# A transformer block in fp32 halves on one core: order of PE, ACT and DVE at the head and where one product's end meets the next product's start

## The chip, the cores and the metric

The kernel runs on one core of one Trainium2 chip. The metric is device time in microseconds (us) of one execution; the medians below are over the runs shown. A profiled execution also leaves a trace of every instruction on TensorE (PE, with weight loads as PEld), VectorE (DVE), ScalarE (ACT), GpSimd (POOL) and SyncE (SP, which here issues DMAs).

## What is computed

A block of depth 1 over 256 tokens of 2048 values (fp32): a gated feed-forward layer, a mixer (a recurrence of 16 heads plus a pooling branch, both gated), and a second feed-forward layer. Each is added to its input.

```python
def _rmsnorm(x, g):
    xf = x.astype(jnp.float32)
    y = xf * lax.rsqrt(jnp.mean(xf * xf, axis=-1, keepdims=True) + NORM_EPS)
    return (y * g.astype(jnp.float32)).astype(x.dtype)

def _swiglu(x, w_gate, w_up, w_down):
    return (jax.nn.silu(x @ w_gate) * (x @ w_up)) @ w_down
...
        f = _swiglu(_rmsnorm(h, ln_ffn1_pre[l]), ffn1_gate[l], ffn1_up[l], ffn1_down[l])
        h = h + MACARON_WEIGHT * _rmsnorm(f, ln_ffn1_post[l])
        mx = _hybrid_mixer(_rmsnorm(h, ln_mix_pre[l]), w_in[l], rwkv_mu[l], rwkv_w0[l],
...
        h = h + _rmsnorm(mx, ln_mix_post[l])
        f = _swiglu(_rmsnorm(h, ln_ffn2_pre[l]), ffn2_gate[l], ffn2_up[l], ffn2_down[l])
        h = h + MACARON_WEIGHT * _rmsnorm(f, ln_ffn2_post[l])
```

The hidden width of the feed-forward layers is 5632, `w_in` has 8480 columns, and the weights are read once.

## The kernel before

**Products.** Each fp32 factor is split into a high half and a low remainder (`xH`, `xL`, `wH`, `wL`), and `mm3` (L126 to L128) makes three matmuls of them: wH with xH, wL with xH, wH with xL. Tokens are 256, in two halves h of 128; a product of 512 output columns has two PSUM tiles of 128x512, one for each half, and runs over k, 128 rows of the weight at a time (16 for an input of 2048, 44 for 5632).

**Weights.** `load_w` issues a DMA on SP for two k of 512 columns (L105; 512 KB) into one of four buffers `w32`, then the cast `wH` on ACT (L108) and the difference `wL` on DVE (L109), each into one of five buffers; where `hold` is set the two go into units of the big pool (`kH`, `kL`) instead.

**Inputs.** `next_pre` makes the transposed input `uT` of the next layer. For each token half h and each 512 columns c it does a turn (`transpose_split`, L257 to L264): four 128x128 transposes on PE into one PSUM tile `tr`, and for each of the four a scaled copy `xH` on ACT (L263) and a scaled difference `xL` on DVE (L264), both reading `tr`. Sums of squares (`sumsq`, L290) and the factor rs (`rstd`) are put off into `s.late`: the product is scaled by rs when it is read out of PSUM.

**The end of a layer.** `post` makes four products of 512 columns. For the last (c == 3), `gemm_tok(trail=True)` does the last 16 k (TRAIL) first for half 0, then for half 1. When a half is done, its evacuation runs: sum of squares on ACT (L290), product with the gain `gb` into `fg` on DVE (L336), one small op on DVE (L349), the power -0.5 on POOL (L352), and four outputs on DVE (L355), each the 512 columns of one turn.

**The start of the next layer.** `gemm_tok(lead=True)` does the first ten k (STAG) of the next product by halves as well. The turns stand in `s.turns` with a time (TURNS, us of PE work after the evacuation), and `by_half` puts a turn among the products when its count has passed that time, or when the product needs it. This happens twice: from the first feed-forward layer to the mixer (`w_out` and `w_in` products around it) and from the mixer to the second feed-forward layer.

**Order.** The framework schedules instructions by priority and by its own model of time. From the trailing product on, `manual_schedule` holds PE alone to the source's order; ACT and DVE are in the scheduler's order there, with raised priorities (BOOST for the splits, FINISH for the turns and evacuations). At the head of the program nothing is held: x comes by eight DMAs on POOL's queue (L1040), the gain's rows and the weights on SP's, all eight turns are in the source ahead of the first product, and the parameters of the mixer are loaded (`setup_mixer`, 12 small DMAs on SP) before the first feed-forward layer.

Of the kernel before, what the change touches and what calls it, by code (L numbers as in the profile page):

```python
# [34 lines left out]
BOOST = 2000  # L35
FINISH = 4000
MM, MC = 0.2265, 0.12
NUNITS = 33
STAG = 10
TRAIL = 16  # L40
TURNS = [[3.8, 5.2, 6.8, 8.6], [4.2, 5.4, 8.8, 10.4]]
TB = 4
# [6 lines left out]
class Block:  # L49
    def __init__(s, tc, ctx):  # L50
        s.tc = tc
        s.nc = nc = tc.nc
        E = ctx.enter_context
        s.n = 0
        s.late, s.turns, s.held = [], [], None
        s.cp = E(tc.tile_pool(name="cp", bufs=1))
        s.wp = E(tc.tile_pool(name="wp", bufs=3))
        s.up = E(tc.tile_pool(name="up", bufs=NUNITS))
        s.tp = E(tc.tile_pool(name="tp", bufs=TB))
        s.sp = E(tc.tile_pool(name="sp", bufs=4))  # L60
        s.dp = E(tc.tile_pool(name="dp", bufs=1, space=bass.MemoryType.DRAM))
        s.pm = E(tc.tile_pool(name="pm", bufs=4, space=PSUM))
        s.pt = E(tc.tile_pool(name="pt", bufs=4, space=PSUM))
        s.ident = s.const([P, P], "ident")
        make_identity(nc, s.ident)
        s.mhalf = s.const([P, 16], "mhalf")
        nc.gpsimd.memset(s.mhalf, -0.5)
# [22 lines left out]

    def load_w(s, w, k0, nk, c0, cw, split=False, hold=False):
        nc = s.nc
        out = []
        step = 1 if split else max(1, 1024 // cw)
        for j in range(k0, k0 + nk, step):
            n = min(step, k0 + nk - j)
            w32 = s.wp.tile([P, 1024], F32, tag="w32", name=s.nm("w32"), bufs=W32_BUFS)
            if hold:
                wH, wL = s.unit(dt=F32R, p="kH"), s.unit(dt=F32R, p="kL")
            else:  # L100
                wH = s.wp.tile([P, 1024], F32R, tag="wH", name=s.nm("wH"), bufs=WS_BUFS)
                wL = s.wp.tile([P, 1024], F32R, tag="wL", name=s.nm("wL"), bufs=WS_BUFS)
            v, vH, vL = [t[:, :n * cw].rearrange("p (k c) -> p k c", k=n)
                         for t in (w32, wH, wL)]
            nc.sync.dma_start(out=v, in_=w[j * P:(j + n) * P, c0:c0 + cw]  # L105
                              .rearrange("(k p) c -> p k c", p=P))
            with s.tc.high_priority(offset=BOOST):
                nc.scalar.copy(vH, v)  # L108
                nc.vector.tensor_tensor(out=vL, in0=v, in1=vH.bitcast(F32), op=ALU.subtract)  # L109
            for i in range(n):  # L110
                out.append((j + i, vH[:, i], vL[:, i]))
        return out
# [16 lines left out]

    def gemm_tok(s, w, c0, at, KT, evac, lead=False, trail=False, first=False):  # L130
        pss = [s.pm.tile([P, 512], F32, tag="mm", name=s.nm("mm")) for _ in range(2)]

        def do(k, wH, wL, h):
            xH, xL = at(k)
            s.mm3(pss[h], xH[:, h * P:h * P + P], xL[:, h * P:h * P + P], wH, wL,
                  k == 0, k == KT - 1)

        def by_half(ws):

            for h in range(2):  # L140
                now = 0
                for k, wH, wL in ws:
                    while s.turns and (s.turns[0][0] <= now or s.turns[0][1] == (h, k // 4)):
                        s.turns.pop(0)[2]()
                    do(k, wH, wL, h)
                    now += 3 * MM
                s.turns = [(t - now, b, f) for t, b, f in s.turns]
                if k == KT - 1:
                    with s.tc.high_priority(offset=FINISH):
                        evac(h, pss[h])  # L150

        def both(k0, k1):
            for k2 in range(k0, k1, 4):
                for k, wH, wL in s.load_w(w, k2, min(4, k1 - k2), c0, 512):
                    do(k, wH, wL, 0)
                    do(k, wH, wL, 1)

        def held(k0, k1):
            ws = []
            for k in range(k0, k1, 2):  # L160
                ws += s.load_w(w, k, 2, c0, 512, first and k < 4, k - k0 >= STAG)
            return ws

        if trail:
            both(0, KT - TRAIL)
            ws = held(KT - TRAIL, KT)
            s.held = s.tc.manual_schedule(engines={mybir.EngineType.PE})
            s.held.__enter__()
            by_half(ws)
            return  # L170
        if lead:
            by_half(held(0, STAG))
            if s.held:
                s.held.__exit__(None, None, None)
                s.held = None
            while s.late:
                s.late.pop(0)()
        both(STAG if lead else 0, KT)
        with s.tc.high_priority(offset=BOOST):
            for h in range(2):  # L180
                evac(h, pss[h])

    def tok_g(s, w, c0, at, KT, evac):
# [49 lines left out]

    def rstd(s, ss, n):
        nc = s.nc
# [4 lines left out]
                                op0=ALU.mult, op1=ALU.add)  # L240
        r = s.small(1, "rs", bufs=8)
        nc.gpsimd.tensor_tensor(out=r, in0=t2, in1=s.mhalf[:, :1], op=ALU.pow)
        return r

# [46 lines left out]

    def ffn(s, wg, wu, wd, uT, rs, gpost, resid, emit, reload, first=False):
        nc = s.nc
        hT = s.new_T(NKF // 4)
        at = s.T_at(uT)
        for b in range(NKF // 4):
# [16 lines left out]

            s.gemm_tok(wg, b * 512, at, NKD, ev_g, lead=(b == 0), first=first and b == 0)
            s.gemm_tok(wu, b * 512, at, NKD, ev_u)
        s.post(wd, s.T_at(hT), NKF, gpost, 0.5, resid, emit, reload)

    def post(s, wd, at, KT, gpost, fac, resid, emit, reload):
# [11 lines left out]
        for c in range(4):  # L330
            def ev(h, ps):
# [7 lines left out]
                if c == 2:  # L339
# [5 lines left out]
                                            op1=ALU.add)  # L345
                if c < 3:
                    return
                r2 = s.small(1, "rt2", bufs=2)
                nc.vector.tensor_scalar(out=r2, in0=ss[h][:, 3:4], scalar1=kf,  # L349
                                        scalar2=part[h], op0=ALU.mult, op1=ALU.add)  # L350
                r = s.small(1, "rs", bufs=8)
                nc.gpsimd.tensor_tensor(out=r, in0=r2, in1=s.mhalf[:, :1], op=ALU.pow)  # L352
                for q in range(4):
                    o = cc_(fg[h], q)
                    nc.vector.scalar_tensor_tensor(out=o, in0=o, scalar=r, in1=resid(h, q),  # L355
                                                   op0=ALU.mult, op1=ALU.add)
                    emit(h, q, o, TURNS[h][q])
            s.gemm_tok(wd, c * 512, at, KT, ev, trail=(c == 3))

    def next_pre(s, gT):  # L360
        uT = s.new_T(4)
        ss = [s.small(4, "ss2") for _ in range(2)]
        rs = [None, None]

        def emit(h, c, ap, at=None):
            def turn():
                with s.tc.high_priority(offset=FINISH):
                    s.transpose_split(ap, uT, c, h, gT)

            def stat():  # L370
                s.sumsq(ap, ss[h][:, c:c + 1])
                if c == 3:
                    rs[h] = s.rstd(ss[h], D)
            s.late.append(stat)
            if at is None:
                turn()
            else:
                s.turns.append((at, (h, c), turn))
        return uT, rs, emit
# [640 lines left out]
def kernel(tc, x, ln_ffn1_pre, ln_ffn1_post, ffn1_gate, ffn1_up, ffn1_down,  # L1020
# [11 lines left out]
    with ExitStack() as ctx:  # L1032
# [3 lines left out]
        def at_tok(u):  # L1036
            return lambda h, c: u[h][c // 2][:, (c % 2) * 512:(c % 2) * 512 + 512]
        for h in range(2):
            for c in range(4):
                nc.gpsimd.dma_start(out=at_tok(xs)(h, c),  # L1040
                                    in_=x[0, h * P:h * P + P, c * 512:c * 512 + 512])
        gr = s.rtmp("g1rows")[:16, :P]
        nc.sync.dma_start(out=gr, in_=ln_ffn1_pre[0].rearrange("(k p) -> k p", p=P))
        ps = s.psum("pg1")
        nc.tensor.transpose(ps[:, :16], gr, s.ident[:16, :16])
        g1 = s.const([P, 16], "g1")
        nc.vector.tensor_copy(g1, ps[:, :16])

        uT, rs, pre = s.next_pre(g1)
        for h in range(2):  # L1050
            for c in range(4):
                pre(h, c, at_tok(xs)(h, c))
        s.setup_mixer(prm)
        uT2, rs2, pre2 = s.next_pre(s.col["ln_mix_pre"])
        xr = [[s.unit(p="xr") for _ in range(2)] for _ in range(2)]
# [10 lines left out]
        def emit1(h, c, ap, at):  # L1066
            pre2(h, c, ap, at)
            nc.gpsimd.dma_start(out=hsp[0, h, :, c * 512:c * 512 + 512], in_=ap)
        s.ffn(ffn1_gate[0], ffn1_up[0], ffn1_down[0], uT, rs, ln_ffn1_post[0],
              at_tok(xr), emit1, load_to(xr, lambda h: x[0, h * P:h * P + P]), first=True)  # L1070
        uT3, rs3, pre3 = s.next_pre(s.col["ln_ffn2_pre"])
        h1 = [[s.unit(p="h1") for _ in range(2)] for _ in range(2)]
# [8 lines left out]
        def emit(h, c, ap, at):  # L1081
            nc.sync.dma_start(out=out[0, h * P:h * P + P, c * 512:c * 512 + 512], in_=ap)
        s.ffn(ffn2_gate[0], ffn2_up[0], ffn2_down[0], uT3, rs3, ln_ffn2_post[0],
              at_tok(h2), emit, load_to(h2, lambda h: hsp[1, h]))
        s.held.__exit__(None, None, None)

# [31 lines left out]
```

## Time and profile before

| | |
|---|---|
| runs shown | 2119.78, 2122.1, 2122.66 us; median 2122.1 |
| the profiled execution | 2122.2 us, its span 2120.5 us |
| granted TensorE clock, mean | 0.995 |
| PE, PEld busy | 2091.8 us (99%), 1761.7 us (83%) |
| DVE, ACT, POOL busy | 1256.8 (59%), 1117.5 (53%), 76.2 us (4%) |
| HBM read, written | 396.69 MB, 8.39 MB |

How to read it: a line of a group has the source line, the engine, the operation, out<-in by the program's names, and the shapes; then busy time and mean ns; then the engine's idle time just before it and what ended most of it ("<-DVE xL L264": the instruction on DVE that wrote xL). A line of the timeline starts with the start and the length in us. PE's matmuls overlap, so a matmul of 0.39 us can start every 0.227 us; idle time and the distance from start to start say more than busy time. PEclk is the share of the full clock that was granted.

### The profile page before, as it was taken

Reading aid. Unit: us, or ns where it says so; the run is one execution under the profiler, and the core shown is the slowest. Engines: PE = TensorE matmul, PEld = TensorE weight load, DVE = VectorE, ACT = ScalarE, POOL = GpSimd, SP = SyncE. Lnnn points to the kernel's source line nnn. Section 1 sums busy time; section 2 is a strip of 40 time slices with the busy share of each in tenths; the row PEclk is TensorE's granted clock in tenths of the full one; section 3 lists DMA queues with packets and bytes.
Section 4 is the critical chain, followed back from the end, with each engine's and each line's share of the span. In section 5 each row is a group of like instructions: output and inputs, shape, how many; then the busy total and the mean of one; then the engine's idle time right before and its main releaser. Section 6 shows DMA issues by size and latency. Waiting matters only on the chain.

```text
span 2120.5 us, 28818 instructions
## 1 busy us (share of the span) xinstructions
PE 2091.8 (99%) x11077; PEld 1761.7 (83%) x11077; DVE 1256.8 (59%) x1588; ACT 1117.5 (53%) x1600; POOL 76.2 (4%) x169
## 2 busy tenths in 40 slices
PE   8999999999999999999999999999999999999998
PEld 6888888888888789989988788878888888888886
DVE  5555555555444555699789666565555555554444
ACT  6565555655444455465465444455655556554442
POOL 1000000000000000000110110000000000000000
PEclk9999999999999999999999999999999999999999
DMA  7666666577666656656456575666566665676664
GB/s 232 196 189 190 200 196 190 178 218 247 191 197 191 214 156 181 180 163 186 138 151 197 151 262 182 194 194 192 178 209 196 192 195 181 212 246 194 193 194 134
DMA packets 223605, 406.99 MB, mean 192 GB/s; under 512 B 13152, under 2 KB 49130, under 8 KB 223466
## 3 DMA queue, kind: packets, MB, share of 16 engines
q1 hardware_dynamic: 216937, 383.11, 59.6%
q0 software_dynamic: 6528, 22.02, 2.9%
q8 instruction: 87, 1.43, 0.3%
q14 instruction: 53, 0.43, 0.1%
HBM read 396.69 MB, written 8.39 MB: 191 GB/s over the span
## 4 chain that ended last, share of the span: by engine, by line
PE 76%; issue 20%; DVE 1%; DMA 1%; ACT 1%; POOL 1%; POOLq 0%; DVEq 0%; SPq 0%; ACTq 0%
PE mm L126 21%; PE mm L128 21%; PE mm L127 21%; PE mc L227 10%; DMA w<-in_ffn_gate_dram 1%; PE pA L840 0%; DVE fg L355 0%; DMA mb<-msp 0%; PE tr L257 0%; ACT x L283 0%; PE pU L936 0%; PE pY L971 0%; PE pSa L948 0%; PE pY L967 0%; PE pM L906 0%
## 5 line engine op out<-in xcount | busy, mean ns | idle before, releaser
L109 DVE TENSOR_TENSOR wL<-w,wH 128x1024 fp32r<-128x1024 f32 (+2 forms) x725 | 872.9, 1211 | 750.2 <-ACT wH L108 748.7
L108 ACT CAST wH<-w 128x1024 fp32r<-128x1024 f32 (+2 forms) x725 | 751.2, 1043 | 833.3 <-PE mm L128 675.6
L126 PE MATMUL mm<-wH,xH 128*128 128x512 f32 x2460 | 965.8, 393 | 6.8 <-ACT xH L263 6.7
L128 PE MATMUL mm<-wH,xL 128*128 128x512 f32 x2460 | 961.6, 391 | 4.4 <-DVE xL L264 4.4
L127 PE MATMUL mm<-wL,xH 128*128 128x512 f32 x2460 | 959.5, 391 | 0.0
L126 PEld LDWEIGHTS mm<-wH,xH 128*128 128x128 f32 x2460 | 463.8, 189 | 104.2 <-ACT xH L263 8.5
L128 PEld LDWEIGHTS mm<-wH,xL 128*128 128x128 f32 x2460 | 463.9, 189 | 102.4 <-DVE xL L264 6.1
L127 PEld LDWEIGHTS mm<-wL,xH 128*128 128x128 f32 x2460 | 463.9, 189 | 94.2
L227 PE MATMUL mc<-xH,wH 128*128 128x256 f32 x560 | 159.9, 285 | 0.0
L227 PE MATMUL mc<-xH,wL 128*128 128x256 f32 x560 | 158.6, 283 | 0.0
L227 PE MATMUL mc<-xL,wH 128*128 128x256 f32 x560 | 158.6, 283 | 0.0
L283 ACT COPY x<-T 32x256 f32<-32x256 f32 x352 | 141.9, 403 | 3.9
L227 PEld LDWEIGHTS mc<-xH,wH 128*128 128x128 f32 x560 | 106.1, 190 | 1.0
L227 PEld LDWEIGHTS mc<-xH,wL 128*128 128x128 f32 x560 | 106.1, 190 | 0.3
L227 PEld LDWEIGHTS mc<-xL,wH 128*128 128x128 f32 x560 | 106.2, 190 | 0.2
L302 ACT ACTIVATE sg<-mm,rs 128x512 f32<-128x512 f32 x44 | 30.1, 690 | 19.9 <-PE mm L128 19.9
L303 DVE SCALAR_TENSOR_TENSOR sg<-mm,rs,sg 128x512 f32<-128x512 f32 x44 | 31.6, 750 | 12.4 <-ACT sg L302 12.3
L333 POOL DMA_DIRECT2D gb<-in_ln_ffn_post_dram x4 | 2.2, 562 | 925.3 <-DVE xL L287 892.0
L290 ACT ACTIVATE junk<-mm 128x512 bf16<-128x512 f32 x24 | 14.3, 596 | 35.2 <-PE mm L128 35.2
L336 DVE TENSOR_TENSOR fg<-mm,gb 128x512 f32<-128x512 f32 x24 | 16.5, 692 | 25.1 <-ACT junk L290 25.1
L308 DVE SCALAR_TENSOR_TENSOR sg<-mm,rs,sg 128x512 f32<-128x512 f32 x44 | 30.9, 742 | 0.0
L273 DVE STREAM_TRANSPOSE T<-sg 128x512 f32<-128x512 f32 x44 | 30.8, 699 | 0.0
(244 smaller groups left out, 1087.6 us busy)
## 6 DMA issues: line engine op xcount, KB each, us to landing
w<-in_ffn_up_dram SPq DMA_DIRECT2D x176, 512.0 KB
w<-in_ffn_down_dram SPq DMA_DIRECT2D x176, 512.0 KB
w<-in_ffn_gate_dram SPq DMA_DIRECT2D x174, 512.0 KB
w<-in_w_in_dram SPq DMA_DIRECT2D x128, 512.0 KB
w<-in_w_out_dram SPq DMA_DIRECT2D x32, 512.0 KB
w<-in_w_proj_b_dram SPq DMA_DIRECT2D x16, 512.0 KB
w<-in_w_proj_a_dram SPq DMA_DIRECT2D x16, 512.0 KB
hsp<-fg POOLq DMA_DIRECT2D x16, 256.0 KB, 3.1
```

Source lines behind the costliest of these rows:

```text
L108: nc.scalar.copy(vH, v)
L109: nc.vector.tensor_tensor(out=vL, in0=v, in1=vH.bitcast(F32), op=ALU.subtract)
L126: nc.tensor.matmul(ps, aH, bH, start=start, stop=False)
L127: nc.tensor.matmul(ps, aH, bL, start=False, stop=False)
L128: nc.tensor.matmul(ps, aL, bH, start=False, stop=stop)
L227: s.nc.tensor.matmul(o, lh, rh, start=one and n == 0, stop=k == KT - 1 and n == 2, skip_group_check=True)
L273: s.nc.vector.transpose(out=T1[:, h * 512:h * 512 + 512], in_=src)
L283: nc.scalar.copy(dst[q * 32:q * 32 + 32, :, :, i], src[i * 32:i * 32 + 32, :, :, q])
L302: nc.scalar.activation(out=sg, in_=ps, func=AF.Sigmoid, scale=rs[h])
L303: nc.vector.scalar_tensor_tensor(out=sg, in0=ps, scalar=rs[h], in1=sg, op0=ALU.mult, op1=ALU.mult)
L308: nc.vector.scalar_tensor_tensor(out=sig[h], in0=ps, scalar=rs[h], in1=sig[h], op0=ALU.mult, op1=ALU.mult)
L336: nc.vector.tensor_tensor(out=cc_(fg[h], c), in0=ps, in1=cc_(gb, c), op=ALU.mult)
```

## The change

ACT and DVE join PE under `manual_schedule`. `gemm_tok` no longer issues the trailing and leading products at once but puts them into a queue (`s.items`, each with its PE time), and weight splits, evacuations, outputs and turns into a heap of events at counted times; `run` goes through both and issues everything in that order. The counted time of four transposes is TT, loads come AHEAD of their first product, and TURNS has new values. The head is written out in `head`, with PE, ACT, DVE and SP in the source's order: x and weights in one queue (SP's) in the order in which they are needed, the weights of the first product in units of their own, and a turn and a split at a time between the products. The sums of squares follow behind the head, `setup_mixer` behind the first block of the first feed-forward layer.

```diff
-TURNS = [[3.8, 5.2, 6.8, 8.6], [4.2, 5.4, 8.8, 10.4]]
+TT = 0.45
+AHEAD = (5.0, 6.0)
+TURNS = [[3.6, 4.7, 5.8, 6.9], [3.6, 4.6, 5.6, 6.6]]
...
+    def at(s, t, fn):
+
+        s.n += 1
+        heapq.heappush(s.events, (t, s.n, fn))
+
+    def run(s):
+
+        E = mybir.EngineType
+        with s.tc.manual_schedule(engines={E.PE, E.Activation, E.DVE}):
+            while s.items or s.events:
+                while s.events and (s.events[0][0] <= s.now or not s.items):
+                    heapq.heappop(s.events)[2]()
+                if s.items:
+                    t, fn = s.items.popleft()
+                    fn()
+                    s.now += t
+            s.stats()
...
+        def by_half(k0, k1, start, ahead):
+
             for k in range(k0, k1, 2):
+                s.at(start + (k - k0) * 3 * MM - ahead,
+                     lambda k=k: keep(s.load_w(w, k, 2, c0, 512, k - k0 >= STAG)))
+            for h in range(2):
+                for k in range(k0, k1):
+                    s.items.append((3 * MM, lambda k=k, h=h: do(k, h)))
+                if k1 == KT:
+                    s.items.append((0, lambda h=h: evac(h, pss[h])))
 
         if trail:
             both(0, KT - TRAIL)
+            s.now = 0.0
+            by_half(KT - TRAIL, KT, 0.0, AHEAD[0])
             return
+        k0 = 0
+        if xs:
+            s.head(w, c0, KT, do, keep, xs)
+            k0 = KT
+        elif lead:
+            by_half(0, STAG, sum(t for t, _ in s.items), AHEAD[1])
+            s.run()
+            k0 = STAG
+        both(k0, KT)
...
+    def head(s, w, c0, KT, do, keep, xs):
+
+        load, turn = xs
+        w32 = {}
+
+        def get(k, n):
+            w32[k] = (n, s.get_w(w, k, n, c0, 512, own=True))
+
+        def split(k):
+            n, t = w32[k]
+            keep(s.two(t, k, n, 512))
+        E = mybir.EngineType
+        with s.tc.manual_schedule(engines={E.PE, E.Activation, E.DVE, E.SP}):
+            load(0, 0)
+            load(None, None)
+            get(0, 1)
+            get(1, 1)
+            load(1, 0)
+            get(2, 1)
+            get(3, 1)
+            for c in range(1, 4):
+                load(0, c)
+                get(4 * c, 2)
+                load(1, c)
+                get(4 * c + 2, 2)
+            split(0)
+            turn(0, 0)
+            split(1)
+            do(0, 0)
+            turn(1, 0)
+            split(2)
+            do(1, 0)
+            split(3)
+            do(0, 1)
+            do(1, 1)
+            do(2, 0)
+            do(2, 1)
+            for c in range(4):
+                k = 4 * c
+                if c < 3:
+                    turn(0, c + 1)
+                    split(k + 4)
+                if c:
+                    for i in range(3):
+                        do(k + i, 0)
+                        do(k + i, 1)
+                        if c < 3 and i == 1:
+                            turn(1, c + 1)
+                            split(k + 6)
+                elif c < 3:
+                    turn(1, c + 1)
+                    split(k + 6)
+                do(k + 3, 0)
+                do(k + 3, 1)
+            s.stats()
...
-                if c < 3:
-                    return
+                if c == 3:
+                    end = s.now
+                    r = s.small(1, "rs", bufs=8)
+                    s.at(end + 0.9, lambda: norm(h, r))
+                    for q in range(4):
+                        s.at(end + 1.7 + 0.7 * q, lambda q=q: out(h, q, r, end))
...
         def emit(h, c, ap, at=None):
             def turn():
-                with s.tc.high_priority(offset=FINISH):
-                    s.transpose_split(ap, uT, c, h, gT)
+                s.transpose_split(ap, uT, c, h, gT())
+                s.now += TT
...
             if at is None:
                 turn()
             else:
-                s.turns.append((at, (h, c), turn))
+                s.at(at, turn)
...
-        for h in range(2):
-            for c in range(4):
-                nc.gpsimd.dma_start(out=at_tok(xs)(h, c),
-                                    in_=x[0, h * P:h * P + P, c * 512:c * 512 + 512])
...
+        def load(h, c):
...
+            nc.sync.dma_start(out=at_tok(xs)(h, c),
+                              in_=x[0, h * P:h * P + P, c * 512:c * 512 + 512])
+
+        def turn(h, c):
+            pre(h, c, at_tok(xs)(h, c))
+        s.after.append(lambda: s.setup_mixer(prm))
```

`get_w` is the DMA of the old `load_w` and `two` its cast and difference; `norm` and `out` are the old small op, power and output of the evacuation.

## Prediction

> **What bounds the kernel now.** I read the page's busy shares first, then PE's stretches, then what PE waited for, then ACT and DVE in order of time at the places found. A "product" below is one 128x512 matmul; a "block" is the three products of one k and one token half; a "turn" is the four transposes of 512 columns with the four xH copies (ACT) and four xL copies (DVE) behind them; a "split" is the cast wH (ACT) and the difference wL (DVE) of one weight load.
>
> ```profile
> PE 2091.8 (99%) x11077; PEld 1761.7 (83%) x11077; DVE 1256.8 (59%) x1588; ACT 1117.5 (53%) x1600; POOL 76.2 (4%) x169
> ```
> ```profile
> 0.00:10.00 10.00, 4.16 (x13) 2.78 (x14) 3.17 (x7) 5.25 (x11) 8.08 (x42) 1.00 0.74 249
> 10.00:20.00 10.00, 6.56 (x27) 4.72 (x26) 6.10 (x19) 7.59 (x26) 0.56 (x1) 0.86 0.93 333
> 20.00:30.00 10.00, 10.00 (x50) 8.12 (x50) 7.69 (x19) 9.19 (x22) 0.56 (x1) 0.97 0.43 113
> 738.25:751.51 13.26, 9.47 (x30) 6.78 (x29) 8.95 (x26) 8.66 (x30) 4.98 (x24) 0.74 0.49 173
> 1384.00:1397.50 13.50, 9.52 (x33) 6.79 (x32) 8.59 (x24) 9.32 (x32) 3.88 (x7) 0.75 0.55 190
> 2110.00:2120.50 10.50, 1.55 (x7) 0.94 (x5) 3.55 (x6) 0.69 (x2) 0.55 (x1) 0.81 0.27 100
> ```
>
> PE is the bound almost everywhere (columns: length, busy time and count of PE, PEld, DVE, ACT, POOL, granted clock, DMA). Only the head, the two places where a product's end meets the next one's start, and the tail have holes. So the change is worth what it does there, and the median (2122.1) and the profiled execution (2122.2 us, span 2120.5) are the same for this sum.
>
> What stands there today, in PE time lost against its own pitch (product to product 0.227 us, four transposes 0.44):
> - Head: the last product of the first gate block starts at 39.8.
> - First transition: from 738.25 to 753.33 PE did 30 products and 8 transposes, 6.8 + 0.9 = 7.7 us of work in 15.1: 7.4 lost. Second: 1384.45 to 1397.65, 24 products and 8 transposes, 6.3 in 13.2: 6.9 lost. Part of both is a halved clock after the holes (0.74, 0.75 in the rows above; products 0.427 apart from 745.8 to 749.7).
>
> The decisive view is ACT and DVE in order of time:
>
> ```profile
> 753.72 0.37 ACT L263 ACTIVATE xH<-tr,cols 128x128 fp32r<-128x128 f32 x1 [0.16 <-DVE xL L264]
> 754.51 0.37 ACT L263 ACTIVATE xH<-tr,cols 128x128 fp32r<-128x128 f32 x1 [0.42 <-DVE xL L264]
> 754.89 1.05 ACT L108 CAST wH<-w 128x1024 fp32r<-128x1024 f32 x1
> ```
> ```profile
> 754.12 0.35 DVE L264 SCALAR_TENSOR_TENSOR xL<-tr,cols,xH 128x128 fp32r<-128x128 f32 x1 [0.18 <-ACT xH L263]
> 754.91 0.35 DVE L264 SCALAR_TENSOR_TENSOR xL<-tr,cols,xH 128x128 fp32r<-128x128 f32 x1 [0.43 <-ACT xH L263]
> 755.97 1.23 DVE L109 TENSOR_TENSOR wL<-w,wH 128x1024 fp32r<-128x1024 f32 x1 [0.71 <-ACT wH L108]
> ```
> ```profile
> 17.29 2.18 ACT L263 ACTIVATE xH<-tr,g 128x128 fp32r<-128x128 f32 x8
> 17.70 2.16 DVE L264 SCALAR_TENSOR_TENSOR xL<-tr,g,xH 128x128 fp32r<-128x128 f32 x8
> ```
>
> Within one turn ACT and DVE alternate: xH waits for the xL before it, one pair per **0.79 us** (753.72 to 754.51). Eight copies in a row take 0.27 each only because the scheduler took them from several turns and put the other turns' copies and the splits into the waits. The built program says the same: each xH after a turn's first waits for the xL before it, although it writes another quarter of the tile; both read one PSUM tile. The Trainium skill, "PSUM — Partial Sum Buffer", section "PSUM bank collisions raise a hardware error", says that ACT and DVE may not read one bank (and partition quadrant) at the same time and that software must order them by semaphores; the 0.42 us waits agree.
>
> **The change, part by part.** The order in which the changed kernel builds differs from the old one only in the head and the two transitions; PE's order at the tail is the old one (0). There ACT and DVE now take a turn's four copies one after the other, in source order. So a turn holds both engines for 3 x 0.79 + 0.35 = 2.72 us on DVE, and its waits hide nothing. Everything queued behind (splits, the evacuation of a product's end) comes late, and PE behind it.
>
> *Head.* Loads: eight x loads leave POOL's queue for SP's, 8 x 0.42 us of issue. The first w load now takes 2.76 us from issue (1.25) to its cast (4.01). So x lands at 0.81 + 2.76 = 3.6 and w0, third in the queue, at about 4.4. From there loads are ahead: at the 333 GB/s of the 10 to 20 row the 3.7 MB that follow x up to the w load of the third chunk are there by about 15, and that load is cast at 27. Loads slower by 1 to 2 us would cost 0.5 to 1.2, faster ones give 0.5.
> - First two turns with their splits: casts of 0.62 and differences of 0.69 between the pairs; DVE is through the first turn at 8.4, the second at 11.95. PE does 15 products, most at 0.427, to 14.7, then the third turn's transposes; ACT, in order, sits before that turn's first xH until 15.4.
> - Then six turns, each with one split of 1024: 3 x 0.79 for the pairs, about 0.97 for the cast (1.05 less overlap), about 1.15 for the difference (1.22 less overlap): 4.5 us, where PE has 4 blocks and 4 transposes, 3.2. From the first xL at 15.8: 15.8 + 6 x 4.5 = 42.8. Eleven products follow: the gate block's last one starts at about 45.2.
> - 45.2 against 39.8; two products of the next block are then done earlier than before (0.45). **+5.0.**
>
> *Each transition*, from the first product of the second half on (725.48 in the old trace, here 0; the second transition has the same order). Evacuation of the first half as now: fg outputs 1 to 3 until 4.4.
> - Turn 1's transposes come after six blocks (4.1); xL pairs until 7.85. Output 4 then until 8.5: turn 4's transposes need it at 7.5, PE waits 1.1.
> - Turn 2's pairs until 11.15, split 1 (cast 10.7 to 11.7, difference to 13.0), turn 3 to 15.6, split 2 (cast to 16.2, difference to 17.5), turn 4 to 20.1, split 3 (cast to 20.7, difference to 22.0), splits 4 and 5 to 24.3. Only then the second half's evacuation: product with gb to 24.9, then as today (+0.8) output 1 from 25.65 to 26.35, 2 and 3 to 27.6; output 4 stands behind turn 1's pairs, 31.2. Today this product ran at 740.43, 14.95 on the same count.
> - PE: second half ends at 10.9 + 4 x 0.44 + 1.1 = 13.8; two blocks to 15.1; the third waits 1.15 for cast 2 and 1.05 for its difference; the fifth 2.1 for cast 3 and 1.05; the next transposes 3.2 for output 1; the last ones 1.9 for output 4. Together **11.6 us** a transition, and a half-speed clock falls into time that PE waits anyway.
> - 11.6 against 7.4 and 6.9: **+4.2 and +4.7.**
>
> *Costs taken as nothing.* The 12 small parameter loads (0.22 to 0.46 each, 4 us of SP) move between weight loads of the second block: casts run up to five buffers, 5 x 2.7 us of PE work, ahead. Eight sums of squares (0.85 each) move behind the head; 18 us of ACT work (8 casts, sums, table load, sigmoids) to about 61, while PE needs the banks back at 45 + 22 = 67. Without that cover each late us would be one us of PE. POOL's pow for the second rstd stands behind 15 one-column memsets of 0.04 us: nothing.
>
> Sum: 5.0 + 4.2 + 4.7 = 13.9; 2122.2 + 13.9 = **2136.1 us**, 0.65% slower. A measurement here can tell about 0.2%, 4.2 us.
>
> **Rivals.**
> 1. *Pairs overlap* (the other side). If a turn's copies ran at 0.27 as in the x8 rows, a turn is 1.1 us. The head's period falls to 2.4, under PE's 3.2: the first gate block ends near 33.9, -6.0 (one wait of 1.05 for the first 1024 split left). In a transition the evacuation product then ends at 17.1 and PE waits 1.9 + 0.25: -5.3 and -4.8. Time 2106. The point of decision: between 0.27 (-16.1) and 0.79 (+13.9) the sum changes sign at about 0.55 us a pair. Against it: the 0.42 and 0.43 waits above, 12 of them in the whole trace. 5%.
> 2. *The clock takes more.* Holes of 1.69 and 2.06 us brought 6.8 us of half clock in each transition today; a 3.2 hole may leave two periods of that behind the last wait, 15 products of +0.2: +3 each, 2142. For: the rows' 0.74. Against: most of the half-speed time lies in further waits. 18%. The Trainium skill, "TensorE: Matmul & The Clock Gate", Part 1, has the gate look at a free-running window of about 3.4 us and halve the clock after an idle one; the 6.8 us here are two of those, and by it this rival depends on where the hole falls.
> 3. *The loads pay for the head.* Today w loads wait for four buffers and share the DMA with POOL's x loads (a hole of 2.8 us ends at 15.72). If the ordered loads bring the first two turns forward by more than I count, the head comes out even: 2131. 14%.
> 4. *It doesn't do what it says*: the built order shows that it does. Loads or splits out of step could leave the time within 0.2%: 3%.
>
> **Numbers.** Forecast 60% (2133 to 2140), rival 2 18%, rival 3 14%, rival 1 5%, rival 4 3%. The range goes from rival 3 with 2 us to spare to rival 2 with 2: 2129 to 2144. Faster by over 0.2%: 5%; within 0.2%: 3%; slower: 92%.
>
> **What will show it.** ACT's waits for xL and DVE's for xH: now 5.4 us in 12 and 10.8 in 16; 24 turns x 3 waits of 0.42 give some 30 us in 72 each. The head's wL differences 4.5 us apart from 20 to 42. New rows in PE's waits, none today: products on wH and wL, transposes on fg (3.2 and 1.9). The second half's evacuation product some 24 us after that half began. If xH copies of one turn start 0.27 apart, or that product comes 15 us in, the working is wrong.

## The result and the profile after

The changed kernel takes **2137.28 us** (median of 4 runs, 2136.39 to 2137.77) beside 2122.03 (2119.78 to 2122.66): ratio 1.0073, 95% interval 1.0056 to 1.0091. The profiled execution took 2136.39 us, its span is 2134.7.

Where the time came from, in PE time lost (the distance from one PE start to the next, less the median distance behind an instruction of that kind, summed over a stretch; for the head the wait for the first transposes of x is added):

| | before | after | difference | forecast |
|---|---|---|---|---|
| head, to 60 us | 5.6 + 9.1 = 14.7 | 4.2 + 15.4 = 19.6 | +4.9 | +5.0 |
| first transition | 7.7 | 11.9 | +4.3 | +4.2 |
| second transition | 7.1 | 12.2 | +5.1 | +4.7 |
| last PE end to the end of the span | 8.9 | 8.5 | -0.4 | 0 |

The four differences make 13.9; the spans differ by 14.2. The busy shares hardly tell it, PE even has more busy time, because matmuls overlap and a slow clock lengthens them:

```profile
PE 2099.6 (98%) x11077; PEld 1763.6 (83%) x11077; DVE 1261.6 (59%) x1588; ACT 1119.9 (52%) x1600; POOL 73.7 (3%) x161
```

Stretches of the changed kernel (length; busy time and count of PE, PEld, DVE, ACT, POOL; granted clock; DMA share; GB/s), the last one the tail:

```profile
10.00:20.00 10.00, 8.16 (x33) 6.16 (x32) 4.63 (x10) 4.61 (x11) 0.00 (x0) 1.00 1.05 391
20.00:30.00 10.00, 8.97 (x35) 7.08 (x36) 5.79 (x13) 4.98 (x11) 0.00 (x0) 0.83 0.57 210
737.87:761.25 23.38, 16.75 (x62) 12.08 (x61) 15.21 (x29) 11.31 (x25) 2.77 (x5) 0.78 0.49 154
1388.51:1413.20 24.69, 17.79 (x66) 12.94 (x65) 16.06 (x31) 11.69 (x26) 3.21 (x6) 0.79 0.46 150
2124.20:2134.70 10.50, 1.98 (x9) 1.31 (x7) 3.55 (x6) 0.69 (x2) 0.55 (x1) 0.77 0.27 100
```

From 20 to 30 PE does 35 instructions where it did 50, with DMA at 0.57 of its share and DVE and ACT busy for 5.8 and 5.0 of 10 us. PE's 8.97 us contain some 3.4 at half clock (the 0.83 of the row). So none of the four is at its limit; they wait for each other. The clock column doesn't tell everything: from 10.59 to 13.15 products start 0.427 apart, about half of the usual pace, under a row that says 1.00.

What waits, in the changed kernel (us in total, times, longest):

```profile
ACT xH L345 <- DVE xL L346: 40.1, 66, 1.3
DVE xL L346 <- ACT xH L345: 32.8, 71, 2.2
```
```profile
PE mm L155 <- ACT wH L131: 7.8, 9, 1.7
PE tr L339 <- DVE fg L445: 5.8, 4, 1.9
PE mm L156 <- DVE wL L132: 5.7, 8, 0.8
```

And in the kernel before:

```profile
ACT xH L263 <- DVE xL L264: 5.4, 12, 1.0
DVE xL L264 <- ACT xH L263: 10.8, 16, 3.4
PE mm L126 <- ACT xH L263: 6.7, 4, 2.8
PE mm L128 <- DVE xL L264: 4.4, 3, 2.1
```

ACT and DVE wait for each other 66 and 71 times, where 72 each were forecast. The three waits of PE for splits and for `fg` are new, as forecast. PE's old waits for xH and xL, 11.1 us together, are down to 0.5. ACT and DVE in order of time in the first transition:

```profile
749.06 0.37 ACT L345 ACTIVATE xH<-tr,cols 128x128 fp32r<-128x128 f32 x1 [0.42 <-DVE xL L346]
749.85 0.37 ACT L345 ACTIVATE xH<-tr,cols 128x128 fp32r<-128x128 f32 x1 [0.42 <-DVE xL L346]
750.11 2.92 ACT L131 CAST wH<-w 128x1024 fp32r<-128x1024 f32 x3
```
```profile
749.46 0.35 DVE L346 SCALAR_TENSOR_TENSOR xL<-tr,cols,xH 128x128 fp32r<-128x128 f32 x1 [0.43 <-ACT xH L345]
750.25 0.35 DVE L346 SCALAR_TENSOR_TENSOR xL<-tr,cols,xH 128x128 fp32r<-128x128 f32 x1 [0.43 <-ACT xH L345]
751.18 3.50 DVE L132 TENSOR_TENSOR wL<-w,wH 128x1024 fp32r<-128x1024 f32 x3 [0.58 <-ACT wH L131]
754.59 0.68 DVE L420 TENSOR_TENSOR fg<-mm,gb 128x512 f32<-128x512 f32 x1
756.08 2.08 DVE L445 SCALAR_TENSOR_TENSOR fg<-fg,rs,xr 128x512 f32<-128x512 f32 x3 [0.68 <-POOL rs L441]
```

The copies of a turn start 0.79 apart on both engines, each behind a wait for the other; three casts then stand ready to run without a break, since they had been queued behind the copies; and the second half's evacuation (L420) comes after all of that. The head has the same picture with a period of 4.43 us:

```profile
23.55 1.22 DVE L132 TENSOR_TENSOR wL<-w,wH 128x1024 fp32r<-128x1024 f32 x1 [0.58 <-ACT wH L131]
27.98 1.22 DVE L132 TENSOR_TENSOR wL<-w,wH 128x1024 fp32r<-128x1024 f32 x1 [0.58 <-ACT wH L131]
```

### The profile page after: what moved, and what is told of

The parts are those of the page before. It is cut to its first block, busy times and chain, and to the rows that moved or that the text cites. A ratio compares the mean times of both kernels' runs of the same rounds, so it can differ in the third digit from the quotient of the medians.

```text
span 2134.7 us, 28779 instructions
## 1 busy us (share of the span) xinstructions
PE 2099.6 (98%) x11077; PEld 1763.6 (83%) x11077; DVE 1261.6 (59%) x1588; ACT 1119.9 (52%) x1600; POOL 73.7 (3%) x161
## 4 chain that ended last, share of the span: by engine, by line
PE 95%; issue 2%; DVE 1%; ACT 1%; DMA 0%; POOL 0%; SPq 0%; DVEq 0%; POOLq 0%; ACTq 0%
PE mm L155 27%; PE mm L156 27%; PE mm L157 27%; PE mc L311 10%; PE tr L339 1%; DVE xL L346 0%; ACT xH L345 0%; PE pA L930 0%; ACT wH L131 0%; DVE wL L132 0%; PE pU L1026 0%; DVE fg L445 0%; PE pSa L1038 0%; PE pY L1061 0%; PE pY L1057 0%
## 5 line engine op out<-in xcount | busy, mean ns | idle before, releaser
L345 ACT ACTIVATE xH<-tr,cols 128x128 fp32r<-128x128 f32 x64 | 22.6, 366 | 41.7 <-DVE xL L346 25.2
L384 ACT ACTIVATE sg<-mm,rs 128x512 f32<-128x512 f32 x44 | 30.1, 689 | 21.9 <-PE mm L157 21.9
L385 DVE SCALAR_TENSOR_TENSOR sg<-mm,rs,sg 128x512 f32<-128x512 f32 x44 | 31.7, 751 | 9.0 <-ACT sg L384 9.0
L372 ACT ACTIVATE junk<-mm 128x512 bf16<-128x512 f32 x24 | 14.3, 597 | 37.5 <-PE mm L157 37.5
L346 DVE SCALAR_TENSOR_TENSOR xL<-tr,cols,xH 128x128 fp32r<-128x128 f32 x64 | 22.0, 349 | 20.1 <-ACT xH L345 20.1
L420 DVE TENSOR_TENSOR fg<-mm,gb 128x512 f32<-128x512 f32 x24 | 16.5, 692 | 27.2 <-ACT junk L372 27.2
```

Source lines behind the costliest of these rows:

```text
L345: nc.scalar.activation(out=dH[:, i], in_=ps[:, i], func=AF.Copy, scale=g)
L346: nc.vector.scalar_tensor_tensor(out=dL[:, i], in0=ps[:, i], scalar=g, in1=dH[:, i].bitcast(F32), op0=ALU.mult, op1=ALU.subtract)
L384: nc.scalar.activation(out=sg, in_=ps, func=AF.Sigmoid, scale=rs[h])
L385: nc.vector.scalar_tensor_tensor(out=sg, in0=ps, scalar=rs[h], in1=sg, op0=ALU.mult, op1=ALU.mult)
```

## The experiments

Theory A is the prediction's: xH and xL of one turn alternate because they read one PSUM tile (128x512), and with ACT and DVE held in source order nothing fills the waits. The rivals are that PE's new order or the order of loads costs the time, that the clock does, and that the pitch of 0.79 us isn't due to the shared tile.

**Undoing the order, part by part.** Three kernels hold less.

```diff
-        with s.tc.manual_schedule(engines={E.PE, E.Activation, E.DVE}):
+        with s.tc.manual_schedule(engines={E.PE}):
```

> The changed kernel, but at the two transitions only PE is held in the written order; ACT and DVE there are ordered by the scheduler, as in the kernel before. The head is untouched. Theory A (alternating pairs, held in source order, leave waits that nothing fills): the scheduler puts other turns' copies and the splits into those waits, the lost PE time of a transition falls from 12.0 and 12.1 us to about the 7.6 and 7.1 of the kernel before, so 2137.3 - 9.4 = about 2128; ACT's waits for xL fall from 66 to about 24 (the 8 turns of the head), DVE's likewise. Rival 'PE's own new order costs it': the transitions stay near 12 us each and the time at 2137. Rival 'the clock takes more': the stalls go, but a halved clock stays for 10 us after them, so that only about half comes back, 2132 to 2133.

Measured: 2127.12 us, 1.0022 of the kernel before (1.0012 to 1.0032), so 10.2 of the 15.3 us are gone. The transitions lose 8.1 and 7.0 us, ACT waits for xL 30 times instead of 66. DVE at the first transition:

```profile
735.50 3.48 DVE L132 TENSOR_TENSOR wL<-w,wH 128x1024 fp32r<-128x1024 f32 x3
740.56 1.12 DVE L346 SCALAR_TENSOR_TENSOR xL<-tr,cols,xH 128x128 fp32r<-128x128 f32 x4
745.71 0.68 DVE L420 TENSOR_TENSOR fg<-mm,gb 128x512 f32<-128x512 f32 x1
```

Four xL take 1.12 us here, with one tile a turn: the scheduler put other work first and mixed the copies of several turns, so that neighbours in the row come from different tiles (ACT did one xH each of four turns at 735.67, 736.28, 737.93 and 738.54, before the first xL at 738.91). The evacuation comes at 745.71, 9 us earlier.

```diff
-        with s.tc.manual_schedule(engines={E.PE, E.Activation, E.DVE, E.SP}):
+        with s.tc.manual_schedule(engines={E.PE, E.SP}):
```

> The changed kernel, but at the head only PE and SP (the loads) are held in the written order; ACT and DVE there are ordered by the scheduler. Transitions untouched. Theory A: the period of the head's splits falls from 4.43 us to PE's 3.2, the last gate product starts at about 40 instead of 45, time 2137.3 - 5 = about 2132. Rival 'the loads in one queue set the head': nothing comes back, the differences stay 4.4 us apart, 2137.

Measured: 2133.22 us (1.0053, 1.0041 to 1.0066), 4.1 less than the changed kernel. The direction is A's, the size somewhat less than 5. In the profiled run the head loses 17.2 instead of 19.6, and the loss has another shape: the scheduler puts x's sums of squares and casts ahead of the first xH, and PE, still in the written order, stands for 7.2 us before its first products:

```profile
PE mm L155 <- ACT xH L345: 7.2, 1, 7.2
```

After that the differences come fast enough. So an order for PE alone, without one for the engines that feed it, has a price of its own at the head.

> Both of the above: PE and, at the head, SP in the written order; ACT and DVE ordered by the scheduler everywhere. Theory A: the two parts add up, 2137.3 - 9.4 - 5 = about 2123, the time of the kernel before within 3 us; whatever stands above that is PE's new order or the loads. Rival 'PE's order and the loads cost it': 2130 or more.

The edit is both of the above. Measured: 2123.93 us (1.0009, 1.0000 to 1.0018): 13.4 us gone, and the two parts add up (10.2 + 4.1 = 14.3). What PE's new order and the loads cost or bring together is about 2 us (0 to 3.8 by the interval). The order of ACT and DVE made the rest.

**The queue of x.**

```diff
-            nc.sync.dma_start(out=at_tok(xs)(h, c),
+            nc.gpsimd.dma_start(out=at_tok(xs)(h, c),
```

> The changed kernel with the eight x loads on POOL's queue again, everything else as changed. Theory A: the head is set by the alternating pairs, 4.43 us a turn, so the queue matters only for when the first turn starts: within 1.5 us of 2137.3. Rival 'the loads in one queue pay for the head': without them the head is later by the 1 to 5 us that they had brought forward, 2139 to 2142. Rival 'one queue costs': 2133 to 2135, since w0 then is first in its queue.

Measured: 2138.61 us (1.0079, 1.0066 to 1.0091), 1.3 more than the changed kernel. The first xL starts at 7.48 instead of 5.97 and the first 1024-wide difference at 20.43 instead of 19.12, so the 1.3 are a later start and nothing more. The loads in one queue do bring the head forward, but by far less than the rival needed.

**The shared tile.** All engines stay held, in the same order; only the tiles change.

```diff
-        ps = s.psum("tr").rearrange("p (k t) -> p k t", k=4)
-        for i in range(4):
-            nc.tensor.transpose(ps[:, i], src[:, i * P:(i + 1) * P], s.ident)
...
+            pss = [s.psum("tr") for _ in range(2)]
+            ps = [pss[i % 2][:, i // 2 * P:i // 2 * P + P] for i in range(4)]
+            for i in range(4):
+                nc.tensor.transpose(ps[i], src[:, i * P:(i + 1) * P], s.ident)
```

> The changed kernel, all engines held in the same written order, but the four transposes of a turn go to two PSUM tiles in alternation (chunk i to tile i mod 2) instead of one. Theory A (xH waits for the xL before it only because both read one PSUM tile): xH of chunk i+1 no longer waits for xL of chunk i, only that of chunk i+2 does, so one period of 0.79 us carries two pairs, about 0.4 us a pair. By the straight line between the record's two ends (0.27 us a pair gives 2106, 0.79 gives 2136) that is 2106 + 30 x 0.13/0.52 = about 2113. Rival 'the tile isn't what makes them wait' (the order itself, or the engines' own times): no change, 2137.

Measured: 2115.43 us, 0.9972 of the kernel before (0.9961 to 0.9983): 21.9 us less than the changed kernel, faster than the old one, and 2.4 above the 2113 of the expectation. ACT and DVE in order of time at the head:

```profile
24.09 0.62 ACT L346 ACTIVATE xH<-tr,g 128x128 fp32r<-128x128 f32 x2 [1.02 <-DVE xL L347]
24.61 1.04 ACT L131 CAST wH<-w 128x1024 fp32r<-128x1024 f32 x1
```
```profile
23.71 0.60 DVE L347 SCALAR_TENSOR_TENSOR xL<-tr,g,xH 128x128 fp32r<-128x128 f32 x2
24.49 0.61 DVE L347 SCALAR_TENSOR_TENSOR xL<-tr,g,xH 128x128 fp32r<-128x128 f32 x2 [0.18 <-ACT xH L346]
```

The copies go in twos: two pairs in 24.49 - 23.71 = 0.78 us, 0.39 a pair, as A has it. With four tiles (the same edit with 4 in place of 2):

> As before, with four PSUM tiles for a turn, one for each transpose. Theory A: no xH waits for an xL any more, a turn's copies run at about 0.3 us a pair, a turn is 1.1 to 1.5 us; the head's period falls below PE's 3.2 us and the transitions lose about 2 to 4 us each: 2106 to 2109, faster than the kernel before. ACT's waits for xL go to nearly nothing. Rival 'the tile isn't what makes them wait': 2137. Rival 'four tiles of PSUM for one turn starve the rest' (transposes waiting for free tiles): new PE waits on tr, 2115 or more.

Measured: 2111.65 us, 0.9955 of the kernel before (0.9942 to 0.9968), the fastest version here and the one to keep. The head:

```profile
24.15 1.14 ACT L346 ACTIVATE xH<-tr,g 128x128 fp32r<-128x128 f32 x4 [1.13 <-PE tr L343]
```
```profile
24.55 1.13 DVE L347 SCALAR_TENSOR_TENSOR xL<-tr,g,xH 128x128 fp32r<-128x128 f32 x4 [0.28 <-ACT xH L346]
```

Four pairs in 1.13 us, (1.13 - 0.35) / 3 = 0.26 apart, and ACT now waits for PE's transposes, so PE sets the pace. ACT's waits for xL are gone. The time came out 3 to 6 us above the expectation. The prediction's sum for overlapping pairs, 2106 (its first rival), shows where: it gave 1.9 + 0.25 = 2.15 us a transition and 14.7 - 6.0 = 8.7 for the head; the trace has 4.3, 4.0 and 4.15 + 6.2 = 10.4, which is 5.7 more. Part of it is the price of the tiles, which the expectation had as a rival with too high a cost: the pool has four, one turn takes them all, and the next turn's transposes wait.

```profile
PE tr L343 <- DVE xL L347: 3.1, 6, 0.6
```

The Trainium skill, "PSUM — Partial Sum Buffer", section "PSUM bank collisions raise a hardware error", says that engines in different banks don't collide. The three kernels agree, as far as copies from different tiles do overlap: a pitch of 0.79 us with one tile, 0.39 with two, 0.26 with four.

**The tile or the order of issue?** The last test keeps one tile for a turn and all engines held, and mixes two turns at the head.

```diff
-                    turn(0, c + 1)
-                    split(k + 4)
+                    s.wait = []
+                    turn(0, c + 1)
+                    turn(1, c + 1)
+                    p, s.wait = s.wait, None
+                    for i in range(4):
+                        p[0](i)
+                        p[1](i)
+                    split(k + 4)
+                    split(k + 6)
```

> The changed kernel, one PSUM tile for a turn as changed, all engines held; at the head, from the second chunk on, the two token halves' turns are taken together: eight transposes, then the copies pair by pair from one turn and the other in alternation, then both splits. Theory A (a pair waits only for the pair before it in its own tile): two turns take 8 x 0.4 = 3.2 us instead of 2 x 2.75, a chunk 2.3 to 1.3 us less than the present 8.86, of which the later first split gives some back: 2137.3 - 2 to 5, 2132 to 2135. ACT's waits for xL fall from 66 to about 50. Rival (the engines' own times set the pitch of 0.79, whatever tile): 2137 or more.

Measured: 2130.70 us (1.0042, 1.0028 to 1.0055), 6.6 less than the changed kernel, a little more than A's 2 to 5; ACT waits for xL 51 times. DVE at the head:

```profile
16.22 3.15 DVE L348 SCALAR_TENSOR_TENSOR xL<-tr,g,xH 128x128 fp32r<-128x128 f32 x8 [2.16 <-ACT xH L347]
19.94 2.36 DVE L133 TENSOR_TENSOR wL<-w,wH 128x1024 fp32r<-128x1024 f32 x2 [0.58 <-ACT wH L132]
```

Eight copies in 3.15 us, (3.15 - 0.35) / 7 = 0.40 apart, in written order and with the old tiles. The pitch of 0.79 thus belongs to neighbours in one tile, not to the engines and not to the hold as such. The expectation left out that the two splits together also save a wait of 0.58 between them.

**What the written order is worth with four tiles.**

> The four PSUM tiles, with ACT and DVE at the transitions ordered by the scheduler (PE alone held there), the head held. Theory A: with pairs that no longer wait, source order and the scheduler's order differ little: within 3 us of the four-tile kernel, 2104 to 2111. Rival 'the written order itself costs': faster than the four-tile kernel by over 4 us.

The edit is e1's in the four-tile kernel. Measured: 2124.41 us (1.0013, 1.0004 to 1.0022), 12.8 more than with the order held. The expectation missed, and so did the reason behind it: that the order wouldn't matter once pairs overlap. The transitions lose 9.7 and 9.3 us. DVE in the first one, and what PE waits for in the whole run:

```profile
727.41 3.49 DVE L132 TENSOR_TENSOR wL<-w,wH 128x1024 fp32r<-128x1024 f32 x3
730.82 2.34 DVE L347 SCALAR_TENSOR_TENSOR xL<-tr,cols,xH 128x128 fp32r<-128x128 f32 x8
```
```profile
PE tr L343 <- DVE xL L347: 10.7, 11, 3.5
```

The scheduler puts three differences ahead of the first xL. With one tile a turn, three more turns fit into the pool meanwhile; with four, PE's next transposes stand until the copies are through.

```diff
-                s.transpose_split(ap, uT, c, h, gT())
+                with s.tc.high_priority(offset=4000):
+                    s.transpose_split(ap, uT, c, h, gT())
```

> The kernel of e7 (four PSUM tiles for a turn, ACT and DVE at the transitions ordered by the scheduler), with the turns' transposes and copies ranked above the weight splits for the scheduler (at the head nothing changes, it is held). e7 came out at 2124.4 where 2104 to 2111 was expected; its trace shows three wL differences (3.49 us, from 727.41) ahead of the first xL (730.82), and transposes that wait 3.5 us for an xL to free their tile. Theory B (the scheduler's rank, splits above copies, costs e7 its time): with the copies first the transitions lose about what e6 lost (4.3 and 4.0 instead of 9.7 and 9.3), 2124.4 - 10.7 = about 2114. Rival (the scheduler's order loses against a written one whatever the rank): 2120 or more.

Measured: 2125.17 us (1.0013, 1.0004 to 1.0022). Theory B in that form falls: DVE still does three differences (3.49 us from 726.21) ahead of the first xL (729.61), so a rank above the splits doesn't move the copies ahead of them. By what the scheduler chose this order stays open.

> The kernel before, with four PSUM tiles for a turn and nothing else. It tells what the written order is worth once pairs no longer wait. Theory A: the old kernel waits for xL and xH only 5.4 us in 12 and 10.8 us in 16 in all, so the tiles can bring it little: each transition at most its stalls of 1.97 and 2.24 us, 2122 - 2 to 8, 2114 to 2120, and it stays slower than e6 (2111.65). Rival (the tiles are everything, the order nothing): 2111 to 2112. Rival (the scheduler holds tiles too long, as in e7): 2122 or more.

The edit is the four tiles in the old kernel. Measured: 2121.18 us, ratio 0.9997 (0.9988 to 1.0006): no difference, where 2 to 8 us less were expected. Its transitions lose 7.3 and 6.4. PE's waits for xH and xL (6.7 and 4.4 us before) are gone; in their place its transposes wait 6.9 us for an xL to free their tile (5 times, longest 2.8), and its products 3.2 us for splits. Together:

| medians, us | ordered by the scheduler | ACT and DVE held too |
|---|---|---|
| one tile a turn | 2122.0 (before) | 2137.3 (the change) |
| four tiles a turn | 2121.2 (e9) | 2111.7 (e6) |

The left column is the old kernel's whole order, the right one the changed kernel's. Tiles alone bring nothing, this written order alone costs 15 us (mixed as in e10, some 9), both together gain 10.

## Why the prediction was right, point by point

- **The mechanism** (a turn holds ACT and DVE for 3 x 0.79 + 0.35 us, and in source order nothing fills it): shown. e1 to e3 take the order away and the time comes back, e5, e6 and e10 take the shared tile away from neighbours and the pitch falls to 0.39, 0.26 and 0.40.
- **Head**, +5.0: measured +4.9. w0 was cast at 4.71 (about 4.4 forecast), DVE was through the first turn at 8.67 (8.4), the third turn's first xH came at 15.43 (15.4), the period was 4.43 (4.5), the last difference of the gate block ended at 42.5 (42.8). The start, 0.3 us late, was made up by the third turn, and six periods 0.07 shorter each put the last difference 0.3 ahead of the forecast.
- **Transitions**, 11.6 each: measured 11.9 and 12.2. Counted from the second half's first product (730.62), the evacuation product ended at 755.27, +24.65 (24.9 forecast), and output 4 at 761.80, +31.2 (31.2).
- **PE's waits in a transition** were right as a list up to the last two. In the first one, excess of the start-to-start distances beside the forecast wait: turn 4's transposes 1.16 (1.1), cast 2 and its difference 0.90 and 1.03 (1.15, 1.05), cast 3 and its difference 1.91 and 1.03 (2.1, 1.05), the next transposes 2.32 (3.2). The last wait, 1.9 for output 4, shrank to some 0.2. These stalls make 8.4 us; the other 3.6 are for the most part products at half clock, 0.427 apart, and transposes at half clock. The sum held because output 4 sets the end: PE, at half speed, arrived later and had less to wait for. The step "a half-speed clock falls into time that PE waits anyway" is what carried it.
- **Costs taken as nothing**: between 60 and 700 us PE lost no time before or after (the count differs by 0.2 us), so the moved parameter loads and sums of squares were covered. The tail gave 0.4 us that wasn't forecast.
- **Rival 1** (pairs overlap): false for this kernel, and its price was tested: e6 is that case, 5.6 us above its 2106.
- **Rival 2** (the clock takes more, +3 each): the half clock did grow, from 6.8 to 10.2 us in each transition, but cost little on top, for the reason above: some 0.3 us, which DVE's first xL after the evacuation waited (0.28) behind transposes at half clock. That it was the clock is worked out from the trace; no run isolates it.
- **Rival 3** (the loads pay for the head): e4 puts the worth of the one queue at 1.3 us, too little to bring the head out even.

## What to carry to other kernels

Before holding two engines to a written order, look for pairs that alternate on a shared buffer: an order with such waits in it has to say what fills them; one that doesn't came out 15 us behind the scheduler's here. Splitting the buffer and fixing the order belong together: here each alone brought nothing or a loss, and both together a gain. When buffers are split, count how many are left for the next user, since the wait may only move to the engine that fills them.

## What was not expected of the hardware

The clock halves after holes that are shorter than the half-speed time that they bring. Windows of the changed kernel in the first transition:

```profile
746.00:749.30 3.30, 1.79 (x7) 1.05 (x6) 2.01 (x4) 1.59 (x4) 0.00 (x0) 1.00 0.33 91
749.30:751.00 1.70, 0.16 (x1) 0.00 (x0) 0.70 (x2) 1.28 (x3) 0.00 (x0) 0.99 0.82 266
751.00:761.20 10.20, 7.61 (x22) 5.62 (x23) 7.75 (x13) 4.35 (x10) 2.23 (x4) 0.50 0.68 227
```

A stretch with two waits of under 0.8 us and one of 1.74 was followed by 10.24 us at half clock (three times 3.41, by the trace's record of the clock), though PE was busy for three quarters of it; the kernel before had 6.83 (twice 3.41) after holes of 1.69 and 2.06. In e6, whose longest excess in a transition is 0.81 us, the clock reads 1.00 through both. The Trainium skill, "TensorE: Matmul & The Clock Gate", Part 1, gives one idle window of about 3.4 us as what halves the clock, and one busy window as what restores it. The multiples of 3.41 agree. If an idle window is one in which PE does nothing at all, the holes don't, since none of them here is that long. Nor does the longest hole alone set how long the half clock lasts: in e5 PE stood once for 3.0 us in each transition, and 3.41 us at half clock followed. By what measure the clock is halved stays open.
